# FFN norm factors moved between the products of the second FFN pair, and elementwise work moved from GpSimd to VectorE

## The chip, the cores and the metric

The kernel runs on one core of one Trainium2 chip. The metric is the device time of one execution in microseconds, taken as the median of repeated runs. The engines are named as the profile names them: PE (TensorE), DVE (VectorE), ACT (ScalarE), POOL (GpSimd), SP (SyncE, which here only issues DMAs).

## The reference, cut to what matters

One decoder layer on x of shape 1024 x 1024 (float32). The change touches its second half, the channel mixer:

```python
x = x + merged @ w_out[l]                       # the output projection and its residual
gu = rmsnorm(x, ffn_norm_g[l]) @ w_up[l]        # 1024 -> 2 * 2816
gate, up = gu[..., :D_FF], gu[..., D_FF:]
gate = causal_depthwise_conv3(gate) + conv_b
x = x + (gelu(gate) * up) @ w_down[l]

def rmsnorm(x, g, eps=1e-6):
    return x * rsqrt(mean(x * x, axis=-1) + eps) * g
```

The norm's factor is one number for each position (row of x). It commutes with the product by w_up, so it can be multiplied in after the product.

## The kernel before, in words

Everything is held transposed: 128 channels on the partitions, 1024 positions along the free axis, in two halves j = 0 and 1 of 512. A float32 product is made of three fp32r matmul passes: each operand is split into a high part, cast by ACT (L96 or L922), and a low part, the difference, by a DVE or POOL instruction (L97 or L923); `mm3` (L186) then issues high x high, low x high, high x low.

**The order of the stages around the change.** `strassen_full` computes the output projection (`wo`), with weights `fw` and activations `ft`, in blocks of 512 x 512. As each block of x1 (the new x) is finished by the adds at L832, `done1` queues what the FFN needs of it: a store to DRAM (L934), its square (L942) accumulated into `ssb` by a DMA that adds into its destination (`accumulate`, L104, issued by POOL), and its operand `hb`, scaled by the norm's gain. There are two sums of squares, one for each half of the positions: `ssb_1308` for j = 1 and `ssb_1273` for j = 0. Each takes one plain write and seven accumulating DMAs; one accumulation waits for the landing of the one before it into the same sum.

**FFN pair 0** multiplies one gate tile and one up tile of w_up with the eight `hb` blocks directly: 96 matmuls, half j = 1 (banks `b_6733`, `b_6734`) and j = 0 (`b_6833`, `b_6834`). Beside it, `t1` to `t4` in `done1` form the Strassen-Winograd sums of the activations (L956, L961, L962, L969) and split them into the operands T1 to T4. **Pairs 1 to 21** are `strassen_pair`s: seven products of 12 matmuls each, in the order A11 x B11, S1 x T1, S2 x T2, A12 x B21, S3 x T3, A22 x T4, S4 x B22. `prepare` (L224) loads a pair's two weight tiles r1, r2, makes the sums s1, s2 of their blocks (L232 to L235) and splits r1, s1, a22 and s2 into A, S and their high and low parts. The change's words count the pairs from one; in the code's count from zero, the weights of the "second and third" pair are those of f = 1 and f = 2.

**The norm's factors.** `rms4a` sums a half's squares over the partitions by four matmuls against a column of ones (L138), then scales (L158), takes a square root on ACT (L123) and refines on DVE (L124, L129 to L131). `rms4b` spreads the factors over the partitions by four matmuls with the identity (L146), and ACT copies them to `RB` (L148). `ffn_act` multiplies the products by `RB` (`times_r`, L351, on POOL) before the convolution. So only L351 needs the factors, not the products.

What is issued in which order on each engine is the framework's work: it arranges the instructions by its own estimate of times, keeps each engine's queue in that order, and inserts semaphore waits. Every engine runs its queue in order.

Of the kernel before, what the change touches and what calls it, by code (L numbers as in the profile page):

```python
# [15 lines left out]
ALU = mybir.AluOpType  # L16
# [6 lines left out]
NH = 512  # L23
DFF = 2816
FT = DFF // P
# [22 lines left out]
def trunk_kernel(  # L48
# [19 lines left out]
    nc = tc.nc  # L68
# [14 lines left out]
    def a4(shape=None, dt=F32, n="a"):  # L83
        return ap_.tile(shape or [P, S], dt, tag="a", name=nm(n))
# [7 lines left out]
    def tiny(n, tag, bufs=4):  # L92
        return sm.tile([P, n], F32, tag=tag, name=nm(tag), bufs=bufs)
# [5 lines left out]
    def half(j):  # L99
        return slice(j * NH, (j + 1) * NH)  # L100
# [33 lines left out]
    def ss_cols(ps, sq, nt, nk, k):  # L134

        for t in range(nt):
            c = t * nk + k
            nc.tensor.matmul(ps[:, c:c + 1], lhsT=sq[:, t * P:(t + 1) * P], rhs=ones[:, 0:1],  # L138
                             start=True, stop=True)
# [14 lines left out]
    def rms4a(sq, pool):  # L154
        ps = pool()
        ss_cols(ps, sq, 4, 1, 0)
        t = tiny(4, "ssum")
        nc.vector.tensor_scalar(out=t, in0=ps[:, :4], scalar1=1.0 / D, scalar2=1e-6, op0=ALU.mult, op1=ALU.add)  # L158
        return rsqrt(t, 4)

    def rms4b(r, hs, pool):
        bcast_rows(r, 4, RB[:, hs], pool)
# [13 lines left out]
    def op1(src, n="op", eng=None):  # L176
        t = a4([P, 2, NH], F32R, n)
        split(t[:, 0, :], t[:, 1, :], src, eng)
        return t[:, 0, :], t[:, 1, :]
# [41 lines left out]
            if (kt // 4, j) != (0, 1):  # L221
                self.T[kt % 4]["B%d%d" % (kt // 4 + 1, j + 1)] = self.b[kt][j]

    def prepare(src):  # L224

        r1, r2 = w4(n="r1"), w4(n="r2")
        nc.sync.dma_start(out=r1, in_=src[0])
        nc.sync.dma_start(out=r2, in_=src[1])
        a11, a12, a22, a21 = r1[:, :NH], r1[:, NH:], r2[:, :NH], r2[:, NH:]
        s1, s2 = w4(n="s1"), w4(n="s2")  # L230
        sub = ALU.subtract
        nc.gpsimd.tensor_tensor(out=s1[:, :NH], in0=a21, in1=a22, op=ALU.add)  # L232
        nc.gpsimd.tensor_tensor(out=s1[:, NH:], in0=s1[:, :NH], in1=a11, op=sub)
        nc.gpsimd.tensor_tensor(out=s2[:, :NH], in0=a11, in1=a21, op=sub)
        nc.gpsimd.tensor_tensor(out=s2[:, NH:], in0=a12, in1=s1[:, NH:], op=sub)  # L235
        A11, A12 = op2(r1, w4, "A")
        S1, S2 = op2(s1, w4, "S")
        t = w4([P, 2, NH], F32R, "A22")
        split(t[:, 0, :], t[:, 1, :], a22)
        A22 = (t[:, 0, :], t[:, 1, :])  # L240
        S3, S4 = op2(s2, w4, "S")
        return A11, A12, A22, S1, S2, S3, S4
# [8 lines left out]
    def strassen_pair(src, h, alloc_ps, mid=lambda: None):  # L251

        A11, A12, A22, S1, S2, S3, S4 = prepare(src) if isinstance(src, bass.AP) else src

        def prod(ps, w, tn, first, more):
            for j in range(4):
                mm3(ps, wsl(w, j), h.T[j][tn], first and j == 0, j == 3, more)

        def add(o, ps, c):
            nc.vector.tensor_tensor(out=o, in0=ps, in1=c, op=ALU.add)  # L260

        b1 = alloc_ps()
        prod(b1, A11, "B11", True, True)
        c_1 = c2()
        nc.scalar.copy(c_1, b1)
        b3 = alloc_ps()
        prod(b3, S1, "T1", True, True)
        prod(b1, S2, "T2", False, True)
        c_2 = c2()
        nc.scalar.copy(c_2, b1)  # L270
        mid()
        F1 = a4(n="F1")
        b2 = alloc_ps()
        prod(b2, A12, "B21", True, False)
        add(F1[:, :NH], b2, c_1)
        mid()
        prod(b1, S3, "T3", False, True)
        c_3 = c2()
        nc.scalar.copy(c_3, b1)  # L279
        F2 = a4(n="F2")  # L280
        add(F2[:, NH:], b3, c_3)
        mid()
        b4 = alloc_ps()
        prod(b4, A22, "T4", True, False)
        add(F2[:, :NH], b4, c_3)
        mid()
        prod(b3, S4, "B22", False, True)
        add(F1[:, NH:], b3, c_2)
        return F1, F2
# [58 lines left out]

    def times_r(F, eng=None):

        (eng or nc.gpsimd).tensor_tensor(out=F, in0=F, in1=RB, op=ALU.mult)  # L351

# [128 lines left out]
    for j in range(2):  # L481
        a = wk[:, W_LAM + 128 * j:W_LAM + 128 * j + 64]
        b = wk[:, W_LAM + 128 * j + 64:W_LAM + 128 * j + 128]
# [115 lines left out]
    def store_qk(i, Fs):  # L599
        for n_, F in enumerate(Fs):  # L600
            times_r(F)
            hi, lo = a4(dt=F32R, n="qh"), a4(dt=F32R, n="ql")
            sc = -0.125 if n_ == 0 else 1.0
            nc.scalar.mul(hi, F, sc)
            nc.vector.scalar_tensor_tensor(out=lo, in0=F, scalar=sc, in1=hi.bitcast(F32),
                                           op0=ALU.mult, op1=ALU.subtract)
# [3 lines left out]
    for i in range(NHEAD - 1):  # L610
        ops = prepare(w_qk[1 + i])
# [299 lines left out]
    hh = Act()  # L911
    stat = {}
# [14 lines left out]
    def done1(d, j):  # L927
        blk = x1[d][:, half(j)]
        i, g1, g2 = d % 4, col(C_GF + d % 4), col(C_GF + 4 + d % 4)
        n1 = ngain[:, i:i + 1]  # L930
        STT = nc.vector.scalar_tensor_tensor

        def store():
            nc.sync.dma_start(out=x1_d[d, :, half(j)], in_=blk)  # L934

        def square():
            if j not in stat:
                stat[j] = a4([P, NH], n="ssb")
                nc.scalar.activation(out=stat[j], in_=blk, func=AF.Square)
            else:  # L940
                sq = c2("sq")
                nc.scalar.activation(out=sq, in_=blk, func=AF.Square)  # L942
                accumulate(stat[j], sq)

        def operand():
            if (d // 4, j) == (1, 1):
                nc.scalar.mul(blk, blk, g2)
                hh.b[d][j] = op1(blk, "hb")
            else:
                hh.b[d][j] = op_g(blk, col(C_GF + d), "hb")  # L950
            hh.block(d, j)

        b = x1[i][:, :NH], x1[i][:, NH:], x1[i + 4][:, :NH], x1[i + 4][:, NH:]

        def t1():
            nc.gpsimd.tensor_tensor(out=b[0], in0=b[1], in1=b[0], op=ALU.subtract)  # L956
            hh.T[i]["T1"] = op_g(b[0], g1, "T1")

        def t2():

            STT(out=b[1], in0=b[1], scalar=n1, in1=b[3], op0=ALU.mult, op1=ALU.add)  # L961
            STT(out=b[3], in0=b[0], scalar=n1, in1=b[3], op0=ALU.mult, op1=ALU.add)  # L962
            hh.T[i]["T2"] = op1(b[3], "T2", nc.gpsimd)

        def t3():
            hh.T[i]["T3"] = op1(b[1], "T3", nc.gpsimd)

        def t4():
            STT(out=b[2], in0=b[2], scalar=g2, in1=b[3], op0=ALU.mult, op1=ALU.subtract)  # L969
            hh.T[i]["T4"] = op1(b[2], "T4", nc.vector)  # L970

        if (d // 4, j) == (0, 1):
            tprep[0].extend((t1, t2, t3))
            return [store, operand, square]
        if (d // 4, j) == (1, 0):
            tprep[1].append(t4)
            return [store, operand, square]
        return [store, square, operand]

    rs = {}  # L980
# [149 lines left out]
    for t in range(len(tiles) + 3):  # L1130
        hd, i = tiles[min(t, 31)]
# [51 lines left out]
    for n, _ in enumerate(wo):  # L1183
        if n == 18:
            w0 = [load_w(w_up[0, k]) for k in range(2)]
        if n == 22:
            w1 = prepare(w_up[1])
    F0 = [a4(n="F1"), a4(n="F2")]
    for n_, j in enumerate((1, 0)):
        ps = [pb3() for _ in range(2)]  # L1190
        for kt in range(KT):
            for k in range(2):

                mm3(ps[k], wsl(w0[k], kt if k == 0 else (kt + 4) % 8), hh.b[kt][j], kt == 0, kt == KT - 1)
            if kt >= 2:
                for f in tprep[n_][:2]:
                    f()
                    tprep[n_].remove(f)
            if kt == KT - 1:
                for f in tprep[n_]:  # L1200
                    f()
            if (j, kt) == (0, 1):
                rs[1] = rms4a(stat[1], pb3)
            if (j, kt) == (0, 5):
                rms4b(rs[1], half(1), pb3)
        for k in range(2):
            nc.scalar.copy(F0[k][:, half(j)], ps[k])

    def rms_mid():
        rs[0] = rms4a(stat[0], pb3)  # L1210
        yield
        rms4b(rs[0], half(0), pb3)
        yield
        stat.clear()

    def ffn_act(f, F1, F2):
# [123 lines left out]
    rm = rms_mid()  # L1340
# [8 lines left out]

    lp = last_pair()  # L1350
    for f in range(1, FT):
        F = strassen_pair(w1 if f == 1 else w_up[f], hh, pb3, lambda: next(lp if f == FT - 1 else rm, None))
        if f == 1:
            ffn_act(0, *F0)
        if f < FT - 2:
            ffn_act(f, *F)
        prev = F
# [96 lines left out]
```

## Time and profile before

| | us |
|---|---|
| median of 3 runs | 1443.79 (1443.49 to 1449.01) |
| the profiled execution's own time | 1449.65 |
| its span | 1448.0 |
| PE busy | 1364.5 (94%), 6502 matmuls |
| DVE busy | 1013.6 (70%) |
| ACT busy | 651.7 (45%) |
| POOL busy | 644.4 (45%) |

The profile shows one execution. A busy PE is not a PE at full speed: the page gives the granted clock beside it, as a share of 2.4 GHz, so 0.50 is 1.2 GHz. The slices of 100 us between 900 and 1200 have PE busy throughout at clock 1.00; the slice from 700 to 800 us has it busy for 77.8 us at a mean clock of 0.88. That slice holds the end of the output projection, pair 0 and the start of pair 1.

### The profile page before, as it was taken

The numbers are of one execution on the slowest core, as the hardware profiler recorded it, in microseconds if no ns is written. First come the engines' busy times: TensorE is split into PE (matmuls) and PEld (weight loads), VectorE is DVE, ScalarE is ACT, GpSimd is POOL, SyncE is SP. The second block draws the span as 40 slices with busy tenths as digits, with TensorE's granted clock in tenths as the row PEclk, the third lists the DMA queues.
The fourth block names the chain that finished last, engine by engine and source line by source line (L and its number), as shares of the span: only waits on it lengthen the run. The fifth ranks groups of instructions, "written<-read, shape, count | busy, mean of one in ns | idle before, by whom it ended". The sixth has DMA issues, their size and how long they took to land. (4 is left out here: it accounts for less than half of the span.)

```text
span 1448.0 us, 17868 instructions
## 1 busy us (share of the span) xinstructions
PE 1364.5 (94%) x6502; PEld 1137.7 (79%) x6502; DVE 1013.6 (70%) x1482; ACT 651.7 (45%) x1065; POOL 644.4 (45%) x419
## 2 busy tenths in 40 slices
PE   7899999999998989889977799999999999999997
PEld 6699777888887777778765688888888888878786
DVE  8764676444444889967877476877777778986763
ACT  6442244444334767633654443344333445445461
POOL 5523355555553544432245455666666641001014
PEclk9899999999999999999988899999999999999998
DMA  5332154223338976277885022222222238944853
GB/s 184 94 110 88 30 209 154 104 105 112 117 102 252 264 189 190 81 218 177 215 205 117 29 94 81 88 78 83 74 87 88 88 103 305 303 110 132 222 138 120
DMA packets 78256, 200.46 MB, mean 138 GB/s; under 512 B 8206, under 2 KB 17550, under 8 KB 78168
## 3 DMA queue, kind: packets, MB, share of 16 engines
q1 hardware_dynamic: 67800, 180.44, 37.9%
q0 software_dynamic: 10368, 18.88, 7.6%
q8 instruction: 51, 0.84, 0.2%
q14 instruction: 37, 0.30, 0.1%
HBM read 143.70 MB, written 47.46 MB: 132 GB/s over the span
## 5 line engine op out<-in xcount | busy, mean ns | idle before, releaser
L189 PE MATMUL b<-ft,fw 128*128 128x512 f32 (+1 forms) x1308 | 298.0, 388 | 14.8 <-DVE ft L97 6.8
L189 PEld LDWEIGHTS b<-ft,fw 128*128 128x128 f32 x1308 | 243.3, 191 | 66.8 <-DVE ft L97 8.3
L351 POOL TENSOR_TENSOR F<-F,RB 128x1024 f32<-128x1024 f32 x74 | 191.6, 2590 | 165.5 <-DVE F L260 134.7
L189 PE MATMUL b<-hb,Ah 128*128 128x512 f32 x608 | 190.3, 393 | 0.0
L260 DVE TENSOR_TENSOR F<-b,c 128x512 f32<-128x512 f32 x152 | 100.7, 683 | 125.9 <-ACT c L279 72.1
L97 DVE TENSOR_TENSOR Sl<-s,Sh 128x1024 fp32r<-128x1024 f32 x76 | 149.3, 1964 | 42.7 <-PE b L189 24.0
L189 PE MATMUL b<-T,Sh 128*128 128x512 f32 x504 | 154.3, 389 | 0.0
L232 POOL TENSOR_TENSOR s<-r 128x512 f32<-128x512 f32 x38 | 60.9, 1602 | 194.7 <-DMA r<-in_w_up 72.8
L189 PEld LDWEIGHTS b<-hb,Ah 128*128 128x128 f32 x608 | 114.9, 189 | 24.2 <-issue 0.5
L189 PE MATMUL b<-hb,Al 128*128 128x512 f32 x304 | 119.5, 393 | 1.9 <-DVE Al L97 1.9
L96 ACT CAST Sh<-s 128x1024 fp32r<-128x1024 f32 x76 | 79.9, 1052 | 83.4 <-DVE Al L97 52.5
L97 DVE TENSOR_TENSOR Al<-r,Ah 128x1024 fp32r<-128x1024 f32 x38 | 77.0, 2026 | 53.1 <-ACT Ah L96 38.2
L189 PEld LDWEIGHTS b<-T,Sh 128*128 128x128 f32 x504 | 94.6, 188 | 19.7
L189 PE MATMUL b<-T,Sl 128*128 128x512 f32 x252 | 96.9, 389 | 0.0
L189 PE MATMUL b<-hb,Sh 128*128 128x512 f32 x304 | 94.1, 391 | 1.4 <-DVE F L260 1.4
L96 ACT CAST Ah<-r 128x1024 fp32r<-128x1024 f32 x38 | 40.0, 1052 | 100.9 <-PE b L189 98.5
L96 ACT CAST fw<-fr 128x512 fp32r<-128x512 f32 x90 | 54.4, 622 | 64.4 <-DVE fw L97 26.0
L189 PE MATMUL b<-Tl,Sh 128*128 128x512 f32 x204 | 79.4, 389 | 0.0
L189 PE MATMUL b<-Th,Sl 128*128 128x512 f32 x204 | 78.5, 389 | 0.0
L189 PE MATMUL b<-Th,Sh 128*128 128x512 f32 x204 | 78.5, 389 | 0.0
L104 POOL DMA_DIRECT2D ssb<-sq x24 | 21.1, 906 | 117.9 <-ACT sq L171 38.2
L189 PE MATMUL b<-wh,hb 128*128 128x256 f32 x384 | 71.8, 286 | 0.0
(257 smaller groups left out, 2991.7 us busy)
## 6 DMA issues: line engine op xcount, KB each, us to landing
fr<-in_w_down SPq DMA_DIRECT2D x47, 512.0 KB, 4.5
r<-in_w_up SPq DMA_DIRECT2D x42, 512.0 KB, 3.5
r<-in_w_gate SPq DMA_DIRECT2D x24, 512.0 KB, 4.1
g_d<-F SPq DMA_DIRECT2D x24, 512.0 KB, 4.8
act_d<-cv SPq DMA_DIRECT2D x22, 512.0 KB, 2.6
act<-act_d SPq DMA_DIRECT2D x22, 512.0 KB, 7.2
fr<-in_w_out SPq DMA_DIRECT2D x18, 512.0 KB, 4.7
ssb<-sq POOLq DMA_DIRECT2D x24, 256.0 KB, 4.2
```

Of the source, the lines that this page charges most:

```text
L96: nc.scalar.copy(hi, src)
L97: (eng or nc.vector).tensor_tensor(out=lo, in0=src, in1=hi.bitcast(F32), op=ALU.subtract)
L104: nc.gpsimd.dma_start(out=dst, in_=src, accum_op=ALU.add)
L189: nc.tensor.matmul(ps, lhsT=w[a], rhs=x[b], start=first and i == 0, stop=last and i == 2, skip_group_check=more)
L232: nc.gpsimd.tensor_tensor(out=s1[:, :NH], in0=a21, in1=a22, op=ALU.add)
L260: nc.vector.tensor_tensor(out=o, in0=ps, in1=c, op=ALU.add)
L351: (eng or nc.gpsimd).tensor_tensor(out=F, in0=F, in1=RB, op=ALU.mult)
```

## The change

Four things: the first norm's factors (both halves) are computed by `rms_mid` at the four calls of `mid()` in pair 1, where before those of j = 1 were computed inside pair 0 and those of j = 0 in pair 1; t1's subtraction (L956) and the low parts of T2 and T3 go from POOL to DVE (T4's was on DVE already); the four weight sums of f = 1 go to DVE; and those of f = 2 too.

```diff
-    def prepare(src):
+    def prepare(src, eng=nc.gpsimd):
...
-        nc.gpsimd.tensor_tensor(out=s1[:, :NH], in0=a21, in1=a22, op=ALU.add)
-        nc.gpsimd.tensor_tensor(out=s1[:, NH:], in0=s1[:, :NH], in1=a11, op=sub)
-        nc.gpsimd.tensor_tensor(out=s2[:, :NH], in0=a11, in1=a21, op=sub)
-        nc.gpsimd.tensor_tensor(out=s2[:, NH:], in0=a12, in1=s1[:, NH:], op=sub)
+        eng.tensor_tensor(out=s1[:, :NH], in0=a21, in1=a22, op=ALU.add)
+        eng.tensor_tensor(out=s1[:, NH:], in0=s1[:, :NH], in1=a11, op=sub)
+        eng.tensor_tensor(out=s2[:, :NH], in0=a11, in1=a21, op=sub)
+        eng.tensor_tensor(out=s2[:, NH:], in0=a12, in1=s1[:, NH:], op=sub)
...
         def t1():
-            nc.gpsimd.tensor_tensor(out=b[0], in0=b[1], in1=b[0], op=ALU.subtract)
+            nc.vector.tensor_tensor(out=b[0], in0=b[1], in1=b[0], op=ALU.subtract)
...
-            hh.T[i]["T2"] = op1(b[3], "T2", nc.gpsimd)
+            hh.T[i]["T2"] = op1(b[3], "T2")
...
-            hh.T[i]["T3"] = op1(b[1], "T3", nc.gpsimd)
+            hh.T[i]["T3"] = op1(b[1], "T3")
...
-            hh.T[i]["T4"] = op1(b[2], "T4", nc.vector)
+            hh.T[i]["T4"] = op1(b[2], "T4")
...
-            w1 = prepare(w_up[1])
+            w1 = prepare(w_up[1], nc.vector)
...
-            if (j, kt) == (0, 1):
-                rs[1] = rms4a(stat[1], pb3)
-            if (j, kt) == (0, 5):
-                rms4b(rs[1], half(1), pb3)
...
     def rms_mid():
-        rs[0] = rms4a(stat[0], pb3)
-        yield
-        rms4b(rs[0], half(0), pb3)
-        yield
+        for j in (1, 0):
+            rs[j] = rms4a(stat[j], pb3)
+            yield
+            rms4b(rs[j], half(j), pb3)
+            yield
         stat.clear()
...
     for f in range(1, FT):
-        F = strassen_pair(w1 if f == 1 else w_up[f], hh, pb3, lambda: next(lp if f == FT - 1 else rm, None))
+        ops = w1 if f == 1 else prepare(w_up[f], nc.vector if f == 2 else nc.gpsimd)
+        F = strassen_pair(ops, hh, pb3, lambda: next(lp if f == FT - 1 else rm, None))
```

The engines' queues follow. **DVE, from the last adds of the output projection on** (`ft_1333` is the last activation operand that the projection waits for, `hb` the operands of pair 0, `x1` the blocks of x1, `s1`, `s2`, `r1`, `r2` the weights of pair 1). Before:

```order
L832 TENSOR_TENSOR x1_553_3643<-x1_553_3643,b_1271_6182 128x512
L97 TENSOR_TENSOR hb_1330_6592<-x1_557_3647,hb_1330_6592 128x512
L97 TENSOR_TENSOR ft_1333_6603<-ga_1082_5295,ft_1333_6603 128x512
L832 TENSOR_TENSOR x1_554_3644<-x1_554_3644,b_1272_6183 128x512
L97 TENSOR_TENSOR hb_1334_6619<-x1_558_3648,hb_1334_6619 128x512
L923 SCALAR_TENSOR_TENSOR hb_1335_6623<-x1_551_3641,cs_72,hb_1335_6623 128x512
L97 TENSOR_TENSOR Al_1343_6656<-r1_1338_6645,Ah_1342_6655 128x1024
```

Now, in the same place:

```order
L832 TENSOR_TENSOR x1_553_3643<-x1_553_3643,b_1271_6182 128x512
L956 TENSOR_TENSOR x1_551_3641<-x1_551_3641 128x512
L97 TENSOR_TENSOR hb_1330_6592<-x1_557_3647,hb_1330_6592 128x512
L97 TENSOR_TENSOR ft_1333_6603<-ga_1082_5295,ft_1333_6603 128x512
L832 TENSOR_TENSOR x1_554_3644<-x1_554_3644,b_1272_6183 128x512
L232 TENSOR_TENSOR s1_1340_6649<-r2_1339_6646 128x512
L234 TENSOR_TENSOR s2_1341_6650<-r1_1338_6645,r2_1339_6646 128x512
L97 TENSOR_TENSOR hb_1334_6619<-x1_558_3648,hb_1334_6619 128x512
L956 TENSOR_TENSOR x1_552_3642<-x1_552_3642 128x512
L923 SCALAR_TENSOR_TENSOR hb_1335_6623<-x1_551_3641,cs_72,hb_1335_6623 128x512
L956 TENSOR_TENSOR x1_553_3643<-x1_553_3643 128x512
L97 TENSOR_TENSOR Al_1343_6656<-r1_1338_6645,Ah_1342_6655 128x1024
```

The four L956 and the four weight sums of pair 1 now stand among the same DVE instructions as before; in all DVE has 20 instructions more. From this first L956 to the L131 that completes the factors of j = 1, DVE now has 70 instructions: 35 plain ones of 512 columns, 24 with a scalar of 512 columns, 6 of 1024 columns and 5 of at most 4 columns.

**POOL, in the same stretch.** Before (the first row is the second accumulation of j = 1):

```order
L104 DMA ssb_1308_6494<-sq_1323_6561 128x512
L956 TENSOR_TENSOR x1_551_3641<-x1_551_3641 128x512
L232 TENSOR_TENSOR s1_1340_6649<-r2_1339_6646 128x512
L234 TENSOR_TENSOR s2_1341_6650<-r1_1338_6645,r2_1339_6646 128x512
L956 TENSOR_TENSOR x1_552_3642<-x1_552_3642 128x512
L956 TENSOR_TENSOR x1_553_3643<-x1_553_3643 128x512
L104 DMA ssb_1308_6494<-sq_1331_6596 128x512
L233 TENSOR_TENSOR s1_1340_6649<-s1_1340_6649,r1_1338_6645 128x512
L956 TENSOR_TENSOR x1_554_3644<-x1_554_3644 128x512
L235 TENSOR_TENSOR s2_1341_6650<-r1_1338_6645,s1_1340_6649 128x512
L104 DMA ssb_1308_6494<-sq_1336_6638 128x512
L104 DMA ssb_1273_6209<-sq_1355_6707 128x512
```

Now:

```order
L104 DMA ssb_1308_6494<-sq_1323_6561 128x512
L104 DMA ssb_1308_6494<-sq_1331_6596 128x512
L104 DMA ssb_1308_6494<-sq_1336_6638 128x512
L104 DMA ssb_1308_6494<-sq_1349_6682 128x512
L104 DMA ssb_1308_6494<-sq_1351_6693 128x512
L104 DMA ssb_1308_6494<-sq_1353_6700 128x512
L104 DMA ssb_1273_6209<-sq_1355_6707 128x512
L104 DMA ssb_1273_6209<-sq_1357_6714 128x512
L104 DMA ssb_1273_6209<-sq_1359_6721 128x512
L104 DMA ssb_1273_6209<-sq_1361_6728 128x512
L232 TENSOR_TENSOR s1_1428_7197<-r2_1427_7194 128x512
```

POOL's elementwise work is gone from there up to the weight sums of pair 3, and the accumulations, which alternated between the two sums after the first four, now stand as all of j = 1 and then all of j = 0.

**PE.** Before, the column sums of j = 1 stood inside the last block of pair 0 (`hb_1360`), and the matmuls that spread them ahead of pair 1 (`Ah_1342`):

```order
L189 MATMUL b_1378_6833<-hb_1360_6725,wh_1315_6527 128x512
L138 MATMUL b_1380_6847<-ones_79,ssb_1308_6494 128x1 x4
L189 MATMUL b_1378_6833<-hb_1360_6725,wh_1315_6527 128x512
L189 MATMUL b_1378_6833<-hb_1360_6725,wl_1316_6528 128x512
L189 MATMUL b_1379_6834<-hb_1360_6725,wh_1318_6533 128x512 x2
L189 MATMUL b_1379_6834<-hb_1360_6725,wl_1319_6534 128x512
L146 MATMUL b_1388_6901<-ident_74,rs0_1382_6854 128x128 x4
L189 MATMUL b_1389_6921<-hb_1274_6211,Ah_1342_6655 128x512 x2
```

Now those sums stand in pair 1's second product (S1 x T1), and behind its fifth product (S3 x T3) come the matmuls that spread them and the column sums of j = 0:

```order
L189 MATMUL b_1386_6916<-T1_1372_6796,Sh_1344_6659 128x512
L138 MATMUL b_1388_6943<-ones_79,ssb_1308_6494 128x1 x2
L189 MATMUL b_1386_6916<-T1_1372_6796,Sh_1344_6659 128x512
...
L189 MATMUL b_1384_6901<-T3_1377_6828,Sh_1347_6666 128x512 x2
L189 MATMUL b_1384_6901<-T3_1377_6828,Sl_1348_6667 128x512
L146 MATMUL b_1394_6972<-ident_74,rs0_1390_6950 128x128 x4
L138 MATMUL b_1397_6994<-ones_79,ssb_1273_6209 128x1 x4
L189 MATMUL b_1401_7008<-T4_1380_6854,A22_1346_6663 128x512 x3
```

All of pair 0 and the first 19 matmuls of pair 1 now stand ahead of the first matmul that needs a sum of squares. SP's queue and the number and kind of ACT's instructions are unchanged.

## Rows read from the trace of the kernel before

**Rows 1.** Stretches of 100 us: PE, PEld, DVE, ACT, POOL, clock, DMA

```profile
700.00:800.00 100.00, 77.82 (x319) 62.16 (x317) 72.66 (x86) 53.22 (x92) 49.47 (x46) 0.88 0.70 169
...
1000.00:1100.00 100.00, 100.00 (x442) 82.82 (x442) 78.02 (x58) 38.48 (x48) 64.29 (x35) 1.00 0.24 84
```

**Rows 2.** Stretches of 10 us

```profile
750.00:760.00 10.00, 4.41 (x15) 3.25 (x14) 10.00 (x5) 3.56 (x7) 8.16 (x8) 0.73 0.34 84
...
770.00:780.00 10.00, 10.00 (x46) 8.29 (x45) 10.00 (x16) 9.66 (x18) 3.06 (x4) 1.00 1.02 252
780.00:790.00 10.00, 2.93 (x13) 2.08 (x12) 3.27 (x5) 1.98 (x4) 8.53 (x8) 0.77 0.40 77
790.00:800.00 10.00, 4.21 (x13) 3.20 (x13) 6.37 (x2) 1.67 (x3) 9.92 (x8) 0.50 0.24 42
```

**Rows 3.** Timeline of PE: start us, us, what, idle before

```profile
744.32 7.81 PE L189 MATMUL b<-ft,fw 128*128 128x512 f32 x25 [1.91 <-ACT ft L96]
757.71 4.56 PE L189 MATMUL b<-ft,fw 128*128 128x512 f32 x11 [5.59 <-DVE ft L97]
762.11 0.62 PE L189 MATMUL b<-hb,wh 128*128 128x512 f32 x2
...
762.79 0.62 PE L189 MATMUL b<-hb,wh 128*128 128x512 f32 x2
...
791.37 1.86 PE L138 MATMUL b<-ones,ssb 128*128 128x1 f32 x8 [8.44 <-DMA ssb<-sq]
...
803.62 2.07 PE L146 MATMUL b<-ident,rs 128*128 128x128 f32 x8 [8.04 <-DVE rs L131]
...
825.52 0.62 PE L189 MATMUL b<-hb,Ah 128*128 128x512 f32 x2
```

**Rows 4.** Timeline of DVE

```profile
744.99 0.69 DVE L97 TENSOR_TENSOR hb<-x,hb 128x512 fp32r<-128x512 f32 x1
745.59 0.68 DVE L832 TENSOR_TENSOR x<-x,b 128x512 f32<-128x512 f32 x1
...
747.98 9.07 DVE L97 TENSOR_TENSOR hb<-x,hb 128x512 fp32r<-128x512 f32 x1
...
763.35 0.74 DVE L961 SCALAR_TENSOR_TENSOR x<-x,ngain,x 128x512 f32<-128x512 f32 x1
764.01 1.40 DVE L923 SCALAR_TENSOR_TENSOR hb<-x,cs,hb 128x512 fp32r<-128x512 f32 x2
...
769.19 1.21 DVE L97 TENSOR_TENSOR Sl<-s,Sh 128x1024 fp32r<-128x1024 f32 x1
...
792.95 5.97 DVE L97 TENSOR_TENSOR T<-x,T 128x512 fp32r<-128x512 f32 x1 [9.68 <-ACT T L96]
...
803.01 0.16 DVE L129 SCALAR_TENSOR_TENSOR rs<-rs 128x4 f32<-128x4 f32 x1
```

**Rows 5.** Timeline of POOL

```profile
747.79 1.63 POOL L956 TENSOR_TENSOR x<-x 128x512 f32<-128x512 f32 x1
...
754.60 1.89 POOL L233 TENSOR_TENSOR s<-s,r 128x512 f32<-128x512 f32 x1
...
820.91 4.88 POOL L351 TENSOR_TENSOR F<-F,RB 128x1024 f32<-128x1024 f32 x2 [20.86 <-ACT RB L148]
```

**Rows 6.** The accumulations' tile from 715 to 830 us: time to landing

```profile
DMA to landing us min/median/max: 3.3/4.2/9.8
```

**Rows 7.** Chain of waits, 736 to 800 us: start us, us, what

```profile
747.24 0.86 POOL ssb L104
...
769.58 3.89 DMA ssb<-sq
...
773.53 0.47 issue
...
774.02 6.92 DMA ssb<-sq
```

## The prediction

> **What bounds the kernel now.** I read the stretches first. Later, in the Strassen pairs, PE is busy for all of 100 us at clock 1.00, so there only PE's own work counts; from 700 to 800 us it is busy for 77.8 us at clock 0.88 [rows 1]. The finer stretches put the loss at 750 to 760 and 780 to 800 us, where the clock falls to 0.73, 0.77 and 0.50 [rows 2]. PE's timeline names three stops there [rows 3]: 5.59 us up to 757.71 (the last item of the output projection waits for DVE's low part `ft`), 8.44 us up to 791.37 (the column sums of j = 1 wait for an accumulating DMA), and 8.04 us up to 803.62 (the spreading matmuls wait for the factors from DVE). A full-speed matmul follows the last after 0.227 us (three from 762.11 to 762.79) [rows 3].
>
> Behind the stops stands POOL. DVE's `hb` at 747.98 lasts 9.07 us where its neighbour lasts 0.69 [rows 4]; it ends when POOL's run of sums ends, from 747.79 to 756.49 (754.60 + 1.89) [rows 5]. At 792.95 a T split on DVE lasts 5.97 us [rows 4], while POOL is busy for 9.92 of 10 us [rows 2]. And the accumulations wait in POOL's queue between those sums: the chain has issues and landings of `ssb` by turns [rows 7]. None of this has to hold PE up: the factors' first user is POOL's product by RB, at 820.91 [rows 5].
>
> On this stall the Trainium skill ("SBUF — State Buffer", section "Who interferes with whom") says that a DVE instruction with two SBUF inputs and a GpSimd instruction reading SBUF exclude each other, the later one waiting for the whole of the earlier. By that rule alone a DVE instruction would wait for one POOL sum, under 2 us; the first stop (5.6 us, and 2.1 of clock behind it) would not come from this, and the sum below would be 15 us in place of 23. The trace has 9.07 us across a run of POOL's sums, and the measurement decides.
>
> **The change part by part.** The baseline is the profiled execution, 1449.65 us (span 1448.0). All queues are unchanged up to 747 us, so I work forward from there, in before's times, to the end of pair 1. In before, pair 2's first matmul is at 825.52 [rows 3] with 12 matmuls of pair 1 still to come (S4 x B22 stands behind it): 825.52 + 12 x 0.227 = 828.2.
>
> *Sums and splits to DVE.* 20 instructions go to DVE: 4 L956, 8 low parts, 8 weight sums. A plain one costs 0.60 us (744.99 to 745.59), one with a scalar 0.66 (763.35 to 764.01), one of 1024 columns 1.2, a tiny one 0.16 [rows 4]. So 20 x 0.60 = 12 us are added to DVE, against 8.5 + 5.4 us of stretching removed (9.07 and 5.97, less about 0.6 each). POOL is left with DMA issues only until pair 3's sums. Where DVE stands now: from the first L956 at 747.98, 35 x 0.60 + 24 x 0.66 + 6 x 1.2 + 5 x 0.16 = 44.8 us without a pause, so the factors of j = 1 are done at **792.8**. `ft_1333` is only one instruction later in the queue and ends near 749.8, before PE wants it: the 5.59 us stop goes.
>
> *PE without stops.* The 25 matmuls from 744.32 end at 752.13 as before; 11 remain, 2.5 us, to 754.6. Pair 0 is 96 x 0.227 = 21.8, to 776.4: its operands come off DVE ahead of it by the same count (the last `hb` is the 35th of the 70, near 772, wanted at about 775). The first five products of pair 1 are 60 x 0.227 = 13.6, and the four column sums of j = 1 cost 0.9 (half of 1.86 at clock 0.50 [rows 2, 3]): PE stands before the spreading matmuls at **790.9**, and waits there for DVE's 792.8.
>
> *The accumulations.* They are now in one line: seven for j = 1, then four for j = 0, each issued 0.55 us after the last into its sum has landed (773.47 to 774.02: 769.58 + 3.89, then 0.47 and edges [rows 7]). The second is issued at 747.24, as before [rows 7]. From there to the landing of the last there are nine landings, eight hand-overs and one issue of 0.9. A landing takes 3.3 to 9.8 us, median 4.2 [rows 6]; 6.92 was seen while the DMA share was 1.02 [rows 2, 7], and the stores of x1 and pair 2's weights now fall into the chain. I take seven at the median and two at 6.9: 747.24 + 29.4 + 13.8 + 4.4 + 0.9 = **795.7**. By the same rows the sum of j = 1 has landed by 778, and PE wants it at 780.7.
>
> *The factors' new wait.* The column sums of j = 0 stand in PE's queue behind the fifth product; behind them wait A22 x T4, S4 x B22 and all of pair 2. So PE goes on at 795.7: 0.9 for these sums, 24 x 0.227 = 5.4, 1.0 for the second spreading (half of 2.07 [rows 3]). The idle time before it lowers the clock once more: after the 5.59 us stop 11 matmuls took 4.56 us instead of 2.5, after a 1.91 us one 25 took 7.81 instead of 5.7 [rows 3], so 2.1 us either way. Pair 1 ends at 795.7 + 0.9 + 5.4 + 1.0 + 2.1 = 805.1, against 828.2: **23.1 us saved**.
>
> *What I cost at nothing.* The sums of f = 2 on DVE lie inside the 44.8 us. The products by RB on POOL start near 804 instead of 820.9, in front of pair 4's sums; pair 4 starts two pairs (38 us) after 803, so they hold nobody. Each cover, if it fails, costs a stop of a few us at pair 2 or 3. From pair 3 on PE is the bound and keeps what was won.
>
> Profiled: 1449.65 - 23.1 = 1426.5. The runs shown have a median 5.9 us below the profiled execution, and one of them is as long as it. I take the saving off the median: 1443.79 - 23.1 = **1420.7**. If the 5.9 us were lost in just this stretch, 17 would remain.
>
> **The rivals.**
> 1. *The accumulations are quick.* All landings at 4.2 give 790.4, so DVE's 792.8 decides: 792.8 + 1.0 + 0.9 + 5.4 + 1.0, with or without the 2.1 of clock, is 801 to 803: 25 to 27 us saved, 1417 to 1419. With no stop at all, 799.2: 29 us, 1414.8. For it: after 776 us little else is left for the DMA. Against: DVE leaves no slack.
> 2. *A later chain.* Landings at 5.4 us (the mean of 3.89 and 6.92 [rows 7]): 801.1, and the 9.4 us behind it give 810.5: 17.7 us saved, 1426. The same comes out if POOL's ten DMA issues of 0.86 [rows 7] hold DVE as its sums did: 8.6 us later factors, 1427. Against the latter: DVE is busy for 10.00 of 10 us in 770 to 780, with instructions of normal length, while POOL issues them [rows 2, 4].
> 3. *The wait is only moved.* All landings at 6.92: 814.8 + 9.4 = 824.2, 4 us saved, 1440: no difference. Then the change doesn't take the stop away but shifts it to the sums' new place in pair 1.
> 4. *Slower.* One line of accumulations in place of two alternating ones: at 9.8 us each [rows 6] the last lands at 840.7, pair 1 ends at 850.1, 22 us late, 1466. It decides from 7.4 us a landing on: (828.2 - 9.4 - 747.24 - 5.3) / 9. For it: one landing did take that long [rows 6]; against: the DMA share is 0.24 to 0.40 in three of the four stretches shown [rows 2], so most landings meet little traffic.
>
> On the fourth the Trainium skill ("SBUF — State Buffer", the warning in the section "SBUF: two separate sides") says that a DMA issued from GpSimd starves for its descriptors while DVE runs in a two-port mode, and "Who interferes with whom" excepts tensor_tensor, which most of DVE's instructions here are. By the warning alone landings would lengthen with DVE never idle; by the exception they stay. The trace has both 3.89 and 6.92 us beside a full DVE and decides neither, so the rival keeps a small chance.
>
> **How the numbers follow.** The forecast (21 to 25 us saved, 1419 to 1423) gets 0.45, the first rival 0.20, the second 0.22, the third 0.08, the fourth 0.05. A measurement here tells 0.5%, 7.2 us, from no change. Faster is the forecast and the first two rivals, 0.87; no difference 0.08; slower 0.05. The range leaves out the third and fourth rivals for the most part and takes in the best case: 1413 to 1434.
>
> **What would show it.** Right: no `hb` or T on DVE above 1 us between 747 and 792; PE without a stop from 744 to near 790; one stop there of 2 to 5 us, released by L131 or by an accumulation; pair 2 starting near 805; the page's POOL busy lower by some 25 us and DVE's by little. Wrong: a stop of PE in the middle of S1 x T1 (the chain of j = 1 late, rivals 2 to 4); DVE instructions stretched again beside POOL's DMA issues; a stop in pair 2 or 3 on `Sl` or on an F add of L260, which would mean that DVE's backlog runs on. The number is wrong if the landings' mean is outside 4 to 5.5 us.

## The result, and the profile after

The changed kernel takes 1421.88 us (median of 4 runs, 1418.42 to 1423.5), the kernel before beside it 1445.09 (1443.49 to 1449.01): a ratio of 0.9826, 95% interval [0.9806, 0.9845], which is 25 us (22 to 28); the two medians alone lie 23.2 us apart. The prediction was 1420.7. The profiled execution takes 1421.06 us (span 1419.4, before 1448.0). POOL's busy time falls from 644.4 to 621.7 us, DVE's from 1013.6 to 984.9 although DVE has 20 instructions more. Of DVE's 28.7 us less, 22.8 lie behind pair 1 (439.1 us there against 461.9): over the whole span its splits `Sl` and `Al` of the Strassen pairs take 1.50 and 1.39 us in the mean, against 1.96 and 2.03. That saves no time, since that part of the span is as long as before (below).

The stretch of 700 to 800 us of the changed kernel; columns as in [rows 1]:

```profile
700.00:800.00 100.00, 92.93 (x420) 75.81 (x419) 78.54 (x124) 62.30 (x106) 26.92 (x29) 1.00 0.71 174
```

PE is busy for 92.9 us from 700 to 800 us, where it was for 77.8 [rows 1], and at clock 1.00 in place of 0.88. The finer stretches show the same, beside those of [rows 2]:

```profile
750.00:760.00 10.00, 10.00 (x46) 8.10 (x45) 10.00 (x16) 4.77 (x9) 1.72 (x2) 1.00 0.54 108
760.00:770.00 10.00, 10.00 (x46) 8.29 (x45) 10.00 (x15) 9.55 (x17) 2.61 (x3) 1.00 0.82 222
770.00:780.00 10.00, 10.00 (x50) 8.41 (x49) 10.00 (x17) 5.75 (x10) 1.72 (x2) 1.00 0.56 120
780.00:790.00 10.00, 8.05 (x36) 6.30 (x35) 10.00 (x19) 6.14 (x9) 0.86 (x1) 1.00 0.21 36
790.00:800.00 10.00, 9.70 (x55) 8.17 (x54) 6.16 (x11) 2.87 (x5) 5.09 (x4) 1.00 0.24 97
```

DVE is busy for all of the 40 us from 750 to 790. The timeline (DVE, POOL, ACT and PE, in order of time; columns as in [rows 3]) answers to [rows 3 to 5]:

```profile
743.89 8.21 PE L189 MATMUL b<-ft,fw 128*128 128x512 f32 x35 [0.31 <-DVE ft L97]
745.30 0.87 POOL L104 DMA_DIRECT2D ssb<-sq  x1 [9.28 <-ACT hb L96]
746.74 0.69 DVE L956 TENSOR_TENSOR x<-x 128x512 f32<-128x512 f32 x1
747.34 0.69 DVE L97 TENSOR_TENSOR hb<-x,hb 128x512 fp32r<-128x512 f32 x1
...
780.61 0.86 POOL L104 DMA_DIRECT2D ssb<-sq  x1 [2.98 <-DMA ssb<-sq]
784.79 1.28 ACT L123 ACT_TABLE_LOAD   x1
...
787.13 0.58 ACT L270 COPY c<-b 128x512 f32<-128x512 f32 x1
787.76 0.72 PE L189 MATMUL b<-T,Sh 128*128 128x512 f32 x2 [1.95 <-ACT c L270]
...
790.88 0.16 DVE L131 SCALAR_TENSOR_TENSOR rs<-rs,rs 128x4 f32<-128x4 f32 x1
791.09 1.16 PE L146 MATMUL b<-ident,rs 128*128 128x128 f32 x8 [0.30 <-DVE rs L131]
792.09 0.95 PE L138 MATMUL b<-ones,ssb 128*128 128x1 f32 x8
...
799.28 0.71 PE L189 MATMUL b<-hb,Ah 128*128 128x512 f32 x2
800.22 11.82 POOL L351 TENSOR_TENSOR F<-F,RB 128x1024 f32<-128x1024 f32 x4 [1.63 <-ACT RB L148]
```

The three stops of before (5.59, 8.44 and 8.04 us) are gone; behind 744 us, 1.95 and 0.30 are left. `hb`, 9.07 us long before, takes 0.69. The second accumulation, before which nothing was changed, stands 1.94 us earlier than in before (745.30 against 747.24 [rows 7]); so 1.94 us of the 28.6 by which the two spans differ come from ahead of the change. Pair 2 starts at 799.28, which is 801.2 in before's times, against the 828.2 reckoned for before: 27.0 us saved in the stretch. Behind it both run equally long, 620.1 and 619.8 us.

The chain of waits (start, us, what) says what decides now:

```profile
787.28 1.20 DVE Sl L97
...
789.83 1.13 DVE Sl L97
791.09 1.16 PE b L146 x8
792.25 0.79 PE b L138 x8
793.04 5.59 PE b L189 x24
798.63 0.89 PE b L146 x8
```

It is DVE to 791 us and PE behind; no accumulation stands in it, where before issues and landings of `ssb` took turns [rows 7]. The landings are 3.3, 3.6 and 9.6 us (least, median, most; 4.2 median before [rows 6]), and the last is issued at 780.61, so by the median it lands at 784.2, some 8 us before the column sums at 792.09 want it.

### The profile page after: what moved, and what is told of

It reads as the page before. It is cut to its first block, busy times and chain, and to the rows that moved or that the text cites. A ratio compares the mean times of both kernels' runs of the same rounds, so it can differ in the third digit from the quotient of the medians.

```text
span 1419.4 us, 17845 instructions
## 1 busy us (share of the span) xinstructions
PE 1355.5 (96%) x6502; PEld 1130.4 (80%) x6502; DVE 984.9 (69%) x1502; ACT 652.4 (46%) x1065; POOL 621.7 (44%) x399
## 5 line engine op out<-in xcount | busy, mean ns | idle before, releaser
L189 PE MATMUL b<-ft,fw 128*128 128x512 f32 (+1 forms) x1308 | 291.7, 383 | 8.3 <-ACT ft L96 3.1
L189 PEld LDWEIGHTS b<-ft,fw 128*128 128x128 f32 x1308 | 238.9, 188 | 58.3 <-ACT ft L96 3.9
L351 POOL TENSOR_TENSOR F<-F,RB 128x1024 f32<-128x1024 f32 x74 | 206.0, 2785 | 145.9 <-DVE F L260 135.4
L260 DVE TENSOR_TENSOR F<-b,c 128x512 f32<-128x512 f32 x152 | 100.8, 683 | 112.8 <-ACT c L279 68.7
L232 POOL TENSOR_TENSOR s<-r 128x512 f32<-128x512 f32 x36 | 57.0, 1584 | 200.8 <-DMA r<-in_w_up 96.6
L97 DVE TENSOR_TENSOR Sl<-s,Sh 128x1024 fp32r<-128x1024 f32 x76 | 114.0, 1500 | 26.2 <-PE b L189 22.1
L97 DVE TENSOR_TENSOR Al<-r,Ah 128x1024 fp32r<-128x1024 f32 x38 | 52.6, 1385 | 98.2 <-issue 77.7
L97 DVE TENSOR_TENSOR A<-r,A 128x512 fp32r<-128x512 f32 x38 | 74.6, 1964 | 0.9 <-ACT A L96 0.9
```

Of the source, the lines that this page charges most:

```text
L97: (eng or nc.vector).tensor_tensor(out=lo, in0=src, in1=hi.bitcast(F32), op=ALU.subtract)
L189: nc.tensor.matmul(ps, lhsT=w[a], rhs=x[b], start=first and i == 0, stop=last and i == 2, skip_group_check=more)
L232: eng.tensor_tensor(out=s1[:, :NH], in0=a21, in1=a22, op=ALU.add)
```

## The experiments

Ratios are to the kernel before, which was run beside each of these kernels, with 95% intervals; 0.001 is 1.4 us, and an interval reaches some 0.002 to 0.003 either way. "Above the changed kernel" is the difference of two such ratios, so it is uncertain by about 5 us.

| | on POOL again | ratio | us above the changed kernel |
|---|---|---|---|
| factors only moved | all 20 | 0.9973 [0.9956, 0.999] | 21 |
| engines only | none | 0.9925 [0.9899, 0.9951] | 14 |
| 12 sums added on POOL | (12 others) | 0.9917 [0.9889, 0.9945] | 13 |
| low parts of T2, T3 back | 8 | 0.9877 [0.9856, 0.9897] | 7 |
| L956 and sums of f = 1 back | 8 | 0.985 [0.9828, 0.9872] | 3.5 |
| sums of f = 2 back | 4 | 0.988 [0.9858, 0.9901] | 8 |
| four accumulations more | none | 0.986 [0.9843, 0.9877] | 5 |
| factors one `mid()` later | none | 0.9835 [0.9809, 0.9861] | 1 |
| no square root on ACT | none | 0.9844 [0.9826, 0.9862] | 2.5 |
| the changed kernel again | none | 0.9823 [0.9796, 0.9849] | 0 |

**Each half alone.** First the kernel before with the factors moved:

```diff
-            if (j, kt) == (0, 1):
-                rs[1] = rms4a(stat[1], pb3)
-            if (j, kt) == (0, 5):
-                rms4b(rs[1], half(1), pb3)
...
-        rs[0] = rms4a(stat[0], pb3)
-        yield
-        rms4b(rs[0], half(0), pb3)
-        yield
+        for j in (1, 0):
+            rs[j] = rms4a(stat[j], pb3)
+            yield
+            rms4b(rs[j], half(j), pb3)
+            yield
```

> The kernel before with only the factors moved (j = 1 and j = 0 both in pair 1); all sums and low parts stay on POOL. In before's times, whose pair 1 ends at 828.2 us. My theory (the two halves of the change remove different stops): the first stop of 5.59 us and what it costs in clock (2.1 us) stay; pair 0 then runs through to about 784; the products S2 x T2 and S3 x T3 wait for POOL's low parts of T2 and T3 (till about 794.7), and the factors of j = 1 come when DVE gets through beside POOL, about 803.5; behind that only the last two products are left (1.0 + 0.9 + 5.4 + 1.0 + 2.1 us): 814, some 14 us saved, ratio 0.990 (0.987 to 0.993). Rival A (all of the gain comes from taking the elementwise work off POOL): within 3 us of before, ratio 0.998 or more. Rival B (all of it comes from the factors' new place): 25 to 27 us saved, ratio 0.982.

Measured: 0.9973, some 4 us saved where 14 were expected. The interval does not exclude rival A's 0.998; what speaks against rival A is the next run. The timeline (PE, DVE, POOL, ACT):

```profile
745.01 8.23 PE L189 MATMUL b<-ft,fw 128*128 128x512 f32 x35 [0.30 <-DVE ft L97]
751.88 1.78 DVE L923 SCALAR_TENSOR_TENSOR hb<-x,cs,hb 128x512 fp32r<-128x512 f32 x1
757.61 0.51 PE L189 MATMUL b<-hb,wh 128*128 128x512 f32 x1 [2.23 <-DVE hb L923]
...
785.44 5.54 POOL L97 TENSOR_TENSOR T<-x,T 128x512 fp32r<-128x512 f32 x4
788.57 0.62 ACT L96 CAST T<-x 128x512 fp32r<-128x512 f32 x1 [3.61 <-POOL T L97]
789.23 5.95 DVE L97 TENSOR_TENSOR T<-x,T 128x512 fp32r<-128x512 f32 x1 [9.78 <-ACT T L96]
...
795.21 1.14 ACT L96 CAST T<-x 128x512 fp32r<-128x512 f32 x2 [6.02 <-DVE T L97]
...
798.83 0.59 ACT L265 COPY c<-b 128x512 f32<-128x512 f32 x1
799.47 1.22 PE L189 MATMUL b<-T,Sh 128*128 128x512 f32 x2 [10.18 <-ACT c L265]
```

The first stop, which was expected to stay, is not in this profile, although POOL's and DVE's queues are as before there: PE goes through the 35 matmuls that end the output projection, and stops 2.23 and 1.72 us for `hb` in pair 0 instead. Later a longer wait took the place of the one removed: the expectation had S2 x T2 wait for POOL's low parts till about 794.7, and it began at 799.47, held in another way. S2 x T2 accumulates onto the bank that A11 x B11 left, so PE may not begin it before ACT has copied that bank (`c`, L265). ACT's queue runs in order, and ahead of the copy stand casts of T, which wait for POOL's low parts and then for a DVE instruction of 5.95 us. The factors' new place alone is worth little while POOL's work stands where it was.

Then the other half: the changed kernel with the diff above reversed.

> The changed kernel with the factors where they were before (j = 1 inside pair 0, j = 0 in pair 1); all sums and low parts on DVE. My theory: the 5.59 us stop goes, POOL's part is out of the way, but the matmuls that spread the factors of j = 1 still stand ahead of pair 1 in PE's queue, and L131 that completes them now stands behind DVE's backlog, at about 792.5 in before's times; PE gets there at about 777 and stops for 13 to 16 us; from there to the end of pair 1 it takes the 24.6 us that it took before: 817, some 11 us saved, ratio 0.992 (0.989 to 0.995). Rival A (all of the gain comes from taking the work off POOL): 22 to 27 us saved, ratio 0.982 to 0.985, and no stop over 5 us ahead of pair 1. Rival B (all of it comes from the factors' new place): 0 to 5 us saved.

Measured: 0.9925, 11 us saved, as expected. The timeline:

```profile
790.42 0.16 DVE L131 SCALAR_TENSOR_TENSOR rs<-rs,rs 128x4 f32<-128x4 f32 x1
790.64 2.08 PE L146 MATMUL b<-ident,rs 128*128 128x128 f32 x8 [8.51 <-DVE rs L131]
```

PE stops ahead of pair 1 for 8.51 us, not the 13 to 16 expected, since it came there later (a stop of 2.50 us at 772.81, and 9.84 us for the last 35 matmuls of the output projection, at clock 0.83). Rival A, which had 22 to 27 us saved, is out. The two halves alone save 4 + 11 = 15 us, together 25 by the timed ratio: some 10 us, uncertain by about 5, come only with both.

**POOL's sums or its queue?** In `t1` of the changed kernel, behind L956:

```diff
             nc.vector.tensor_tensor(out=b[0], in0=b[1], in1=b[0], op=ALU.subtract)
+            for _ in range(3):
+                nc.gpsimd.tensor_tensor(out=RB[:, :NH], in0=b[0], in1=b[0], op=ALU.add)
```

> The changed kernel with 12 sums of 512 columns added on POOL, three for each block that L956 sums (their result goes to a part of RB that is overwritten later; nobody waits for it). DVE and PE have the same work as in the changed kernel. Theory 1 (POOL's sums hold DVE's instructions up while both read SBUF): some DVE instructions between 747 and 775 us last several us instead of 0.7, DVE gets to the factors 8 to 12 us later, PE stops for that long, ratio to before 0.988 to 0.992 in place of 0.983. Theory 2 (in before only the queue mattered: accumulations stood behind the sums in POOL's order): DVE's instructions keep their length; the accumulations land up to 8 us later, of which 6 us are slack: 0 to 2 us lost, ratio 0.983 to 0.985.

Measured: 0.9917, in the range of theory 1. The timeline (DVE, POOL, PE):

```profile
750.64 1.93 DVE L923 SCALAR_TENSOR_TENSOR hb<-x,cs,hb 128x512 fp32r<-128x512 f32 x1
750.65 2.83 POOL L958 TENSOR_TENSOR RB<-x 128x512 f32<-128x512 f32 x2
752.50 1.52 DVE L956 TENSOR_TENSOR x<-x 128x512 f32<-128x512 f32 x1
...
778.24 0.50 PE L189 MATMUL b<-hb,wh 128*128 128x512 f32 x1 [3.05 <-DVE hb L923]
779.84 0.88 POOL L104 DMA_DIRECT2D ssb<-sq  x1 [2.21 <-DMA ssb<-sq]
...
802.47 0.15 DVE L131 SCALAR_TENSOR_TENSOR rs<-rs,rs 128x4 f32<-128x4 f32 x1
```

DVE's instructions of 512 columns take 1.4 to 2.3 us beside the sums, PE stops five times from 751 us on (0.94 to 3.05 us, 10 us in all) for `hb` and for a copy, and L131 comes 11.6 us later (802.47 against 790.88), while the last accumulation is issued no later than in the changed kernel (779.84 against 780.61; the second at 745.23 against 745.30). So it is the sums themselves that hold DVE, the first theory; the queue is not needed for it. That they do it by reading SBUF, as the theory has it, was not tried apart. No instruction was held for 9 us here, though.

**The groups one by one.** T2's and T3's low parts back on POOL:

```diff
-            hh.T[i]["T2"] = op1(b[3], "T2")
+            hh.T[i]["T2"] = op1(b[3], "T2", nc.gpsimd)
...
-            hh.T[i]["T3"] = op1(b[1], "T3")
+            hh.T[i]["T3"] = op1(b[1], "T3", nc.gpsimd)
```

> The changed kernel with only the low parts of T2 and T3 back on POOL (8 instructions); factors in pair 1, all sums on DVE. My theory (POOL's late instructions hold DVE's splits of T4, as the 5.97 us one of [rows 4], and ACT's copies stand behind those): DVE has 8 x 0.6 = 4.8 us less to do and loses 5 to 6 us to POOL's second four; S2 x T2 waits for POOL's last low part of T2, and the copy of bank b1 comes late on ACT; a stop of 3 to 8 us in pair 1, ratio 0.986 (0.984 to 0.989) in place of 0.983. Rival (the late group is what the kernel with only the factors moved lost its gain to, whole): a stop of about 10 us at S2 x T2 or S3 x T3 as there, ratio 0.990 or more. Other rival (the early group alone counts): 0.982 to 0.984, no stop over 2 us.

Measured: 0.9877, in the expected range and 0.002 short of the rival's, but with a stop nearer to the rival's 10 us than to the 3 to 8 expected:

```profile
782.66 0.58 ACT L1203 COPY F<-b 128x512 f32<-128x512 f32 x1 [8.11 <-POOL T L97]
...
793.12 1.22 PE L189 MATMUL b<-T,Sh 128*128 128x512 f32 x2 [8.98 <-ACT c L265]
```

Here DVE's longest split of a T beside POOL takes 2.31 us, not 5.97; what PE waits for is again the copy of the bank, behind ACT instructions that wait for POOL. That these wait for a buffer which POOL's low part still reads is what the shared pool `a4` in the code suggests; it was not tried.

The early group back on POOL (`nc.vector` to `nc.gpsimd` in L956 and in `w1 = prepare(w_up[1], ...)`):

> The changed kernel with the early group back on POOL: L956 and the four weight sums of f = 1 (8 instructions between 746 and 762 us); low parts and the sums of f = 2 stay on DVE. My theory: the early stops come back as in the kernel with only the factors moved, 0.3 + 2.2 + 1.7 = 4.2 us on DVE's hb; DVE has 4.8 us less to do and loses 6 to 9 us of stretching, so the factors are 1 to 4 us later; nothing large follows in pair 1, since DVE's T splits are not held any more: 4 to 7 us lost against the changed kernel, ratio 0.987 (0.985 to 0.988). Rival (before's loss was the late group alone): 0.982 to 0.984. Other rival (one group is enough to lose it all): 0.990 or more.

Measured: 0.985, the edge of the expected range and not told apart from the changed kernel by the intervals. The profile shows one long stop, and not the three short ones on `hb` that were expected. The timeline:

```profile
748.39 1.62 POOL L956 TENSOR_TENSOR x<-x 128x512 f32<-128x512 f32 x1
748.84 8.77 DVE L97 TENSOR_TENSOR hb<-x,hb 128x512 fp32r<-128x512 f32 x1
...
758.26 4.80 PE L189 MATMUL b<-ft,fw 128*128 128x512 f32 x11 [6.55 <-DVE ft L97]
```

That is before's first stop [rows 3 to 5] again, 6.55 us in place of 5.59, with the 11 matmuls behind it at the lower level of the clock (0.50 from 758 to 762 us; 4.80 us in place of 2.5). This execution is the longest of its four, 1432.80 us with a median of 1426.84, as before's profiled one is longer than its median; how often the long hold occurs is not shown.

The sums of f = 2 back on POOL, and beside it the changed kernel itself:

```diff
-        ops = w1 if f == 1 else prepare(w_up[f], nc.vector if f == 2 else nc.gpsimd)
+        ops = w1 if f == 1 else prepare(w_up[f])
```

> The changed kernel with the four weight sums of f = 2 back on POOL; PE's order is the same, DVE has four instructions less ahead of the factors of j = 1. My theory (what POOL does beside DVE costs DVE more than the instructions that it saves it): the four sums run on POOL from about 781, after the last accumulation is issued, beside DVE's splits of T4 and Al; DVE saves 2.4 us and loses 3 to 5, and the copy of bank b1, which stands on ACT behind the cast Sh of the sums, comes about 1 us later; 1 to 4 us lost, ratio 0.985 (0.983 to 0.986). Rival (POOL is free there, so DVE only gains): the factors come 2.4 us earlier, 0 to 2 us gained, ratio 0.981 to 0.983, better than the changed kernel.

> The changed kernel itself once more, beside the kernel above, as its measure: every theory expects 0.983 (0.981 to 0.985) to before, an accumulation chain with 3.8 us from issue to issue, a stop of about 2 us on ACT's copy c of bank b1 in pair 1, and no instruction on DVE of 128 x 512 that lasts over 1 us between 747 and 790 us.

Measured: 0.988, beside 0.9823 for the changed kernel: some 8 us lost, where 1 to 4 were expected. The timeline of the first (POOL, ACT, PE):

```profile
789.62 1.26 POOL L235 TENSOR_TENSOR s<-r,s 128x512 f32<-128x512 f32 x1
790.92 1.04 ACT L96 CAST Sh<-s 128x1024 fp32r<-128x1024 f32 x1 [6.59 <-POOL s L235]
...
792.50 1.28 ACT L123 ACT_TABLE_LOAD   x1
...
793.91 0.57 ACT L270 COPY c<-b 128x512 f32<-128x512 f32 x1
...
794.53 1.22 PE L189 MATMUL b<-T,Sh 128*128 128x512 f32 x2 [6.73 <-ACT c L270]
```

DVE lost little (its longest T split takes 1.71 us). POOL could start the sums only behind its last accumulation, at 784.91; ACT's cast of them waited 6.59 us, and the copy that PE needed stood behind the cast. The sums of pair 2's weights (f = 2), which starts at 799 us in the changed kernel, so stopped pair 1.

The changed kernel's second profile has a stop of only 0.43 us on that copy, not the 2 expected, and the same end. PE came to the copy some 1.5 us later, since its 35 matmuls at the end of the output projection took 9.83 us instead of 8.21:

```profile
742.80 9.83 PE L189 MATMUL b<-ft,fw 128*128 128x512 f32 x35 [0.31 <-DVE ft L97]
...
786.67 0.73 PE L189 MATMUL b<-T,Sh 128*128 128x512 f32 x2 [0.43 <-ACT c L270]
...
790.01 1.16 PE L146 MATMUL b<-ident,rs 128*128 128x128 f32 x8 [0.30 <-DVE rs L131]
```

**The chain of accumulations.** The changed kernel with

```diff
                 accumulate(stat[j], sq)
+                if j == 0 and d >= 4:
+                    accumulate(stat[j], sq)
```

> The changed kernel with four of j = 0's squares accumulated twice (four accumulating DMAs more, 15 in place of 11; the norm's factors of j = 0 come out smaller). The spacing of the accumulations in the changed kernel is 3.84 us where nothing else holds them; its last one lands at about 784.5 us, and the column sums of j = 0 stand on PE at 792.1. Theory (the chain decides once it is longer than DVE's work, as the prediction had it): the last lands at 784.5 + 4 x 3.84 = 799.9; PE stops for about 8 us ahead of the column sums of j = 0, 8 to 10 us lost, ratio 0.989 (0.988 to 0.990). Rival (what follows has slack, so that the sums' place is not on the path): 0.982 to 0.984.

Measured: 0.986, 5 us above the changed kernel where 8 to 10 were expected. The stop is there, in the place named:

```profile
797.10 0.86 POOL L104 DMA_DIRECT2D ssb<-sq  x1 [3.28 <-DMA ssb<-sq]
...
800.45 1.87 PE L138 MATMUL b<-ones,ssb 128*128 128x1 f32 x8 [6.70 <-DMA ssb<-sq]
```

Its 6.70 us, and 0.9 for the eight sums at half the clock, make 7.6. The timed difference, uncertain by about 5, does not contradict that. So the chain does decide once it is longer than DVE's work; at its real length it has some 8 us to spare.

**What is left.** Two attempts to remove the 1.95 us: the factors one call of `mid()` later, and no square root on ACT (`rsqrt(t, 4, False)` for these factors).

> The changed kernel with the factors one call of mid() later: nothing at the first call, the sums of j = 1 at the second, the spreading of j = 1 and the sums of j = 0 at the third, the spreading of j = 0 at the fourth. My theory: the two stops left in pair 1 (1.95 us at 785.8, where T3's product waits for a copy that stands on ACT behind the table load of the square root, and 0.30 us for L131) go: up to 2.2 us faster than the changed kernel, ratio to before 0.981 to 0.983. Rival (DVE's backlog is what sets the end, and PE only meets it at another place): the same time as the changed kernel within 1 us, with a stop of about 2 us somewhere in pair 1 or 2.

> The changed kernel with these two norm factors' reciprocal square roots on DVE alone (L126 and three Newton steps in place of ACT's square root and one): ACT loses its L123 and the table load of 1.28 us, DVE gets 7 more instructions of 4 columns for each half (0.16 to 0.2 us each, 1.3 us). Theory: the copy c of bank b1 (L270), for which PE stopped 1.95 us at 785.8, stood on ACT behind that table load; it comes 1.5 us earlier and that stop falls to about 0.5 us; the spreading of j = 1 stands later in PE's order, and nothing else waits: 0 to 2 us gained, ratio 0.981 to 0.983. Rival (the copy is held by DVE, through the T4 splits that ACT's casts wait for): the stop stays at 1.9 us or more and the time is that of the changed kernel or up to 1.5 us longer.

Measured: 0.9835 and 0.9844; neither is told apart from the changed kernel, and neither is better. With the factors later, ACT's copy still holds PE for 1.89 us, with no table load ahead of it but a cast that waits for DVE's split of a T, and 1.40 us more are waited for DVE. Without the square root:

```profile
789.54 0.72 PE L189 MATMUL b<-T,Sh 128*128 128x512 f32 x2 [0.59 <-ACT c L270]
...
795.15 0.73 PE L189 MATMUL b<-hb,Sh 128*128 128x512 f32 x2 [2.58 <-DVE F L260]
```

The table load was most of the 1.95 us, as the first theory had it: the copy now starts 39.0 us behind the first L956 (788.91 against 749.89), in the changed kernel 40.4. But PE then waits 2.58 us for an add of L260, in DVE's queue. Both runs fit the rival of the first, that DVE's work is what remains, whichever stop shows it; a kernel with less work on DVE and none of it on POOL was not run.

## Why the prediction was right, and where it was not

*Sums and splits to DVE.* Right. The forecast had 44.8 us without a pause from the first L956 to the factors; they took 44.3 (746.74 to 791.04). No `hb` or T was long, and the first stop fell from 5.59 to 0.31 us. That every execution of before has the 5.59 is not shown: one was profiled, and the kernel with only the factors moved lacks it.

*The rule on ports, weighed in the prediction.* By the Trainium skill ("SBUF — State Buffer", section "Who interferes with whom") DVE waits for one whole GpSimd instruction. The runs show both: 1.4 to 2.3 us beside the 12 added sums, about one sum and DVE's own 0.6, which agrees with it, and 9.07 us in before and 8.77 us with the early group back, across a whole run of sums, which does not. What chooses between them stays open.

*PE without stops.* Nearly. PE was to stand before L146 at 790.9 in before's times and stood there at 792.7 (790.79 + 1.94): the 1.95 us for ACT's copy were not foreseen. In the changed kernel they cost nothing beyond 0.30, as L131 came no earlier. But the same wait is what the low parts or the sums of f = 2 cost on POOL: the prediction priced them by what they do to DVE and did not follow ACT's queue.

*The accumulations.* This is the mis-sized term. The forecast had the last landing at 795.7, from seven landings at 4.2 and two at 6.9; by the median it was at 784.2 + 1.94 = 786.1, 9.6 us earlier. From the second issue to the last there are eight landings, one after another, in 35.3 us, 4.4 for one with all its waits; less 0.55, a landing is at most 3.9 us in the mean, below the 4 to 5.5 outside which the prediction called its number wrong. The 6.92 of before fell where the DMA share was 1.02 [rows 2, 7]; here it is 0.82 and less from 750 on. That the lighter traffic is the reason is not shown: no run changed the traffic alone.

*The wait that decides.* So it was the first rival's case, DVE's 792.8 (measured 792.98), and not the forecast's: the one stop of 2 to 5 us that the forecast had before L146 is 0.30. The lengthened chain shows that the forecast's mechanism is real and only its size was off.

*The clock.* The 2.1 us after the last stop were not paid: the clock stayed at 1.00, with stops of 1.95 and 0.30 us in place of the one of 4.8 that the forecast had. From L131 to pair 2 it took 8.2 us; the forecast's terms for this way, without the clock, make 8.3.

*The sum.* 23.1 us forecast, 27.0 in the profiled stretch: 2.7 of the 3.9 between them is the chain (795.7 against 792.98), 1.1 the clock less the first spreading, which the forecast had before its wait. The timed ratio, 25 us with an interval of 22 to 28, does not tell the two apart.

*How much of the hit is luck.* 1420.7 lies 1.2 us from the measured median, nearer than its terms account for. The chain and the clock were too long by 3.9 us together. On the other side all rows come from an execution of before that is 4.6 us longer than the median beside it (1449.65 against 1445.09), so that they show more to save than the medians do, 23.2. The range and the direction do not rest on that.

*What was costed at nothing.* Right for the changed kernel: POOL's products by RB began at 800.2, and PE is busy for all of 100 us from 800 to 900. Of the signs, POOL's busy time is lower by 22.7 us, as forecast (some 25); DVE's was to be lower by little and is lower by 28.7, most of it behind the stretch.

## What to carry to other kernels

Where one in-order engine is late, look for what stands behind its consumers in their queues: here POOL's work reached PE three ways, through the operands, through DVE's held instructions, and through ACT, whose copy of a bank stood behind a cast that waited for POOL. Two edits that each remove a stop can be worth little alone, 4 and 11 us, and 25 together, because the next wait stands right behind. The chain of DMA waits was sized too long because two of the worst landings of its old place were carried to the new one; the old median alone, 4.2 us, would have come nearer (790.4 for the 786.1 measured).

## What had not been expected of the hardware

Stops of one length cost the clock differently. Ahead of the same 35 matmuls of the output projection the changed kernel stopped 2.45 us and went on at clock 1.00 (8.21 us for the 35); in its second profile it stopped 2.54 us and the 35 took 9.83, at 0.83 in that stretch (0.51, near the lower level of 1.2 GHz, from 744 to 746 us). Two other kernels fall on either side: 2.77 us and 8.23 with the factors only moved, 2.85 us and 9.84 with the engines only. And a DVE instruction that meets a run of POOL's sums is held for one of them or for the whole run, in kernels whose two queues hold the same instructions there: 1.78 us at most for `hb` with the factors only moved, 9.07 in before. POOL's pace tells the two cases apart: its sums start 1.25 us apart while DVE is held (747.79, 749.06, 750.31 and 751.55 in before), about as long as one lasts alone (1.29 at 793 us in the changed kernel), and 1.6 to 1.8 us apart where the two take turns (746.24, 747.87, 749.66 and 751.37 with the factors only moved).
